# A two-layer encoder on one core: the second layer's transfers leave their queue in the program's order

## The chip, the cores and the metric

The kernel runs on one core of a Trainium2 chip. The metric is the device time of that core in microseconds (us), the median of several runs. The core's engines each run a stream of instructions in order: TensorE (PE, matmuls and transposes), VectorE (DVE), ScalarE (ACT), GpSimd (POOL) and SyncE (SP), which in this kernel does nothing but issue DMA transfers. They meet in semaphores.

## The reference

The program is an encoder trunk of two layers over 1024 tokens of width 1024, in float32. Layer 0 has windowed, dense and memory attention. Layer 1, which the change touches, is cut here to what is computed:

```python
def odd_layer(x, mem_n, table, norm_g, w_in, lq1, lk1, lq2, lk2, subln_g, w_mem_kv, w_out, lam_init):
    h = rmsnorm(x, norm_g)
    q1, q2, k1, k2, v, xq, gate = _split(h @ w_in, ODD_SPLITS)
    ...
    y_c = diff_attention_blocked(q1, q2, k1, k2, v, lam, table)   # p = softmax(s + bias); w = p[0] - lam * p[1]
    y_c = rmsnorm(y_c, subln_g) * (1.0 - lam_init)
    y_x = memory_cross_attention(xq, mem_n, w_mem_kv)
    y = jnp.concatenate([y_c, y_x], axis=-1) * jax.nn.silu(gate)
    return x + y @ w_out
```

There are six differential heads (two score maps of 1024 by 1024 each, a value width of 128) and four memory heads over 256 memory tokens.

## The kernel before, in words

**Precision.** Every float32 operand of a matmul is split into a high part and the rest (suffixes h and l), and each product is three matmuls: high by high, high by low, low by high.

**Stages of layer 1.** `run_steps` (L475 to L530) walks a list of steps: eight cross-attention steps (the ramp, about 635 to 760 us), then six heads of eight query blocks each. One step of a head, over the turns of the loop, is this:

- `s1`: scores `sc` in PSUM, four matmuls of 512 columns (L1505) and four for the low part of k (L1514); one DVE operation (L1520) adds the bias (`toep`) and takes the extremes; ACT takes the exponential (L1523).
- `finish`: DVE normalises the two maps and subtracts them into `e` (L1528, L1530, L1532).
- `hop` (`word_copy`, L565): SP copies `e` to `er`, 512 KB, from SBUF to SBUF, so that it may be read as the matmul's own float type.
- `s2` (L574): eight transposes `te` on PE (L580), whose result ACT (L347) and DVE (L348) split into `PT`.
- `s3`, every second step: `oc`, the product with v (L1545, L1547), added into `O` by ACT and DVE (L1550, L1551); then squares, their sums `ssqc` on PE (L1563), the root on ACT and POOL, `rbcc` on PE (L1576), the scaled `O` on DVE (L1578), the gate on POOL (L1581). The last pair of a head stores its output to `ysc` (`store_y`).

**Filler.** Between these pieces PE runs projection jobs of the next head (k, q, v and gate; `proj_jobs`, matmuls `acc` at L329). A job's 2 x 24 matmuls use one weight block; the block of job i+1 is loaded when job i starts (`load_w`, L235): two transfers `wr` of 256 KB, each cast by DVE into `wh` (L241, 0.5 us) and taken from the raw block by POOL into `wl` (L243, 1.3 us). `wr` has two buffers, which it shares with `wor` and `yr`; `wh` and `wl` have four. A job's results leave through `sg` tiles and small transfers `cq` and `ck`.

**Output weights.** Each turn of the loop also calls `early.step` (L250): it stores the last split piece of the output weights (`wo..h`, `wo..l`), loads the next (`wor`), casts it on ACT (L270) and takes the rest on POOL (L271).

**Tail.** In the last head no projections are left. The output weights come back (`woh`, `wol`, `load_wout`), the stored attention output comes back in chunks `yr` (`y_chunk`, L673), which are split into `yh` by ACT (L350) and `yl` by DVE (L351), and PE's filler is a part of the output projection (`pre`, L702, for token tiles 2, 3 and 4, six of eight k each), whose sums are added to `xh` and stored (`xpsc`). The rest of the output projection follows the loop.

**What sets the order.** The program traces its instructions in the order of the loop. A scheduler then orders every engine's stream by a model of when each instruction could run, inside the dependences; the program can add edges that only order. Nearly all transfers go through one queue, SP's, by the helper `dma` (L175 here, L193 after the change; lines up to L1596 stand 18 lower after the change, those behind it 19 lower).

Of the kernel before, what the change touches and what calls it, by code (L numbers as in the profile page):

```python
# [3 lines left out]

# [1 line left out]

# [82 lines left out]
class Jobs:  # L89
# [59 lines left out]
    def drain(self):  # L149
        self.step = 10 ** 9  # L150
        while self._advance():
            pass


@with_exitstack
def encoder_kernel(ctx, tc, A):
# [76 lines left out]
    def load_w(src, after=None, fast=False):  # L233
        his, los = [], []
        for kh in range(2):  # L235
            raw = wp.tile([P, 4, P], F32, tag="wr", name="wr", bufs=2)
            dma(raw, src[:, 4 * kh:4 * kh + 4, :])
            hi = wp.tile([P, 4, P], F32R, tag="wh", name="wh", bufs=4)
            lo = wp.tile([P, 4, P], F32R, tag="wl", name="wl", bufs=4)
            with (tc.issue_after(after[0]) if after else nullcontext()):  # L240
                nc.vector.tensor_copy(hi, raw)  # L241
            with (tc.issue_after(after[1]) if after else nullcontext()):
                (nc.vector if fast else nc.gpsimd).tensor_tensor(out=lo, in0=raw, in1=hi, op=ALU.subtract)  # L243
            his.append(hi)
            los.append(lo)
        return his, los
# [228 lines left out]
    def run_steps(steps, jobs, hooks=None, pace=None):  # L475
        n = len(steps)
        posts = deque()
        p2 = p3 = 0
        finish = None
        for i in range(n + LAG + 1):  # L480
            behind = None
            if jobs is not None:
                jobs.step = i
            if hooks:
                hooks(i)
            if 0 < i <= n and steps[i - 1].hop:
                steps[i - 1].hop()
            if i < n:
                if steps[i].need:
                    jobs.ensure(*steps[i].need)  # L490
                finish = steps[i].s1()
            f = steps[min(i, n - 1)].fill
            if jobs is not None:
                if half[0] and len(wout) >= 8 and jobs.projected():
                    f = pace(i)
                two = f > 1 and p3 < n and p3 + steps[p3].lag + 1 <= i and steps[p3].s3b is not None
                jobs.pull(f - f // 2 - two)
                if hooks:
                    hooks(-1)
            for q in list(posts):  # L500
                q.pop(0)()
                if not q:
                    posts.remove(q)
            if p3 < n and p3 + steps[p3].lag + 1 <= i:
                st, p3 = steps[p3], p3 + 1
                if st.s3 is not None:
                    if st.need3:
                        jobs.ensure(*st.need3)
                    r = st.s3()
                    if r:  # L510
                        posts.append(r)
                    if st.s3b is not None:
                        jobs.pull(two)
                        st.s3b()
            if p2 < n and p2 + steps[p2].lag <= i:
                behind = steps[p2].s2()
                p2 += 1
            if finish:
                with (tc.issue_after(behind.ins) if behind is not None else nullcontext()):
                    finish()  # L520
                finish = None
            if jobs is not None:
                jobs.pull(f // 2)
                if hooks:
                    hooks(-1)
        while posts:
            for q in list(posts):
                q.pop(0)()
                if not q:
                    posts.remove(q)  # L530
# [276 lines left out]
    last = [None]  # L807
# [185 lines left out]
    jobs = Jobs(jl, ld)  # L993
# [73 lines left out]
    steps = x_steps(M, X, gates, 3, lambda h, qb: (Xq[h], qb * P), 0)  # L1067
# [393 lines left out]
    jobs = Jobs(jl, lambda j: load_w(j["src"], fast=j["tag"] in FAST or j["tag"] == "g7"))  # L1461
# [16 lines left out]
    steps = x_steps(M, X, gates, 3, lambda h, qb: (Xq1[(h, qb // 4)], (qb % 4) * P), 1)  # L1478
# [115 lines left out]
        if i < 0:  # L1594
            wout_hook(1, jobs, "g5", r2)

    run_steps(steps, jobs, hooks1, lambda i: 2)
    jobs.drain()
    left.close()
    st1 = ExitStack()  # L1600
    out_proj(1, None, st1)
# [72 lines left out]
```

## Time and profile before

| | us |
|---|---|
| median of 3 runs | 1228.63 |
| lowest, highest | 1226.69, 1229.92 |
| span of the profiled execution | 1228.9 |
| PE busy | 1196.5 |
| DVE busy | 801.1 |
| ACT busy | 663.1 |
| POOL busy | 436.3 |

The profiled execution has no other time beside its span. It lies 0.3 us above the median. In the rows of the profile an engine's row shows start, duration, line and operation, output and input, and in brackets how long the engine stood idle ahead of it and what ended that. SPq rows are SP's transfers at their issue; PEld are weight loads of PE. A window's row has its length, the busy time and count of PE, PEld, DVE, ACT and POOL, the granted PE clock, the busy share of the DMA engines and the GB/s.

### The profile page before, as it was taken

What the parts mean: (1) busy time and instruction counts of PE and PEld (TensorE: products, weight loads), DVE (VectorE), ACT (ScalarE), POOL (GpSimd) and SP (SyncE); (2) the same over time, 40 slices, a digit from 0 to 9 for tenths busy, and PEclk for the clock granted to TensorE, in tenths of its full rate; (3) what the DMA queues carried; (4) which work ended last, traced back from release to release, by engine and by line L of the source; (5) the groups of instructions that cost most, each with busy time, mean ns of one, the idle gap of its engine ahead of it and who ended that gap; (6) DMA issues with size and microseconds to landing.
All of it is one profiled execution on the core that took longest, in us unless ns stands there. A gap on an engine that the chain in (4) does not pass through costs nothing.

```text
span 1228.9 us, 19560 instructions
## 1 busy us (share of the span) xinstructions
PE 1196.5 (97%) x6614; PEld 988.4 (80%) x6614; DVE 801.1 (65%) x1495; ACT 663.1 (54%) x1477; POOL 436.3 (36%) x414
## 2 busy tenths in 40 slices
PE   6999999999999999999999999999999999999997
PEld 5788888888888777888888777777787777777886
DVE  5547665377778878635365866766767767667544
ACT  6248754366667766636157744555545454445332
POOL 5023365366665455437112222333143231301100
PEclk9999999999999999999999999999999999999999
DMA  6664445545465565457645445355363452468354
GB/s 257 200 194 147 163 172 163 166 160 207 163 233 209 208 227 191 151 196 237 186 158 156 153 146 164 121 183 163 124 187 125 153 171 105 149 212 285 121 192 155
DMA packets 114304, 216.70 MB, mean 176 GB/s; under 512 B 13302, under 2 KB 47478, under 8 KB 114204
## 3 DMA queue, kind: packets, MB, share of 16 engines
q1 hardware_dynamic: 114060, 215.25, 52.5%
q8 instruction: 53, 0.87, 0.3%
q14 instruction: 47, 0.39, 0.1%
q10 hardware_dynamic: 144, 0.20, 0.0%
HBM read 87.71 MB, written 39.86 MB: 104 GB/s over the span
## 4 chain that ended last, share of the span: by engine, by line
PE 47%; DVE 2%; DMA 1%; issue 1%; ACT 1%; POOL 0%; POOLq 0%; SPq 0%; DVEq 0%; ACTq 0%
PE acc L329 24%; PE po L702 5%; PE oc L1545 3%; PE sc L1505 3%; PE te L580 3%; PE sc L1514 2%; PE pre L702 2%; PE oc L1547 2%; DMA wr<-in_w_in 1%; PE ssqc L1563 1%; PE ox L656 0%; PE rbcc L1576 0%; PE tv L439 0%; PE sx L543 0%; DVE e L1520 0%
## 5 line engine op out<-in xcount | busy, mean ns | idle before, releaser
L329 PE MATMUL acc<-h,wh 128*128 128x512 f32 x1536 | 499.5, 398 | 1.6 <-DVE h L351 0.8
L329 PEld LDWEIGHTS acc<-h,wh 128*128 128x128 f32 x1536 | 282.4, 188 | 65.7 <-issue 7.9
L329 PE MATMUL acc<-h,wl 128*128 128x512 f32 x768 | 303.8, 396 | 1.5 <-POOL wl L243 1.2
L243 POOL TENSOR_TENSOR wl<-wr,wh 128x512 fp32r<-128x512 f32 x94 | 124.8, 1329 | 286.3 <-DVE wh L241 155.0
L1523 ACT ACTIVATE e<-e,mn 128x1024 f32<-128x1024 f32 x96 | 110.0, 1148 | 117.0 <-DVE mn L1520 116.9
L329 PEld LDWEIGHTS acc<-h,wl 128*128 128x128 f32 x768 | 144.3, 188 | 34.9 <-issue 4.4
L1114 POOL TENSOR_TENSOR e<-e,rz 128x1024 f32<-128x1024 f32 x48 | 91.6, 1910 | 84.2 <-DVE rz L1113 57.8
L1520 DVE CUSTOM_DVE_ANT_0 e<-sc,toep 128x1024 f32<-128x1024 f32 x96 | 113.5, 1218 | 8.0 <-PE sc L1514 7.3
L580 PEld LDWEIGHTS te<-identr,er 128*128 128x128 f32 x896 | 92.2, 143 | 18.8 <-PE sa L543 2.2
L580 PE MATMUL te<-identr,er 128*128 128x128 f32 x896 | 99.9, 246 | 4.3 <-DVE O L1578 1.4
L348 DVE TENSOR_TENSOR PT<-te,PT 128x512 fp32r<-128x512 f32 x112 | 74.3, 687 | 42.8 <-ACT PT L347 39.2
L241 DVE CAST wh<-wr 128x512 fp32r<-128x512 f32 x112 | 58.2, 522 | 42.9 <-PE acc L329 17.3
L348 DVE TENSOR_TENSOR PTl<-te,PTh 128x512 fp32r<-128x512 f32 x112 | 74.0, 684 | 9.4 <-ACT PTh L347 8.9
L1545 PE MATMUL oc<-PT,v 128*128 128x512 f32 x192 | 69.8, 403 | 0.7 <-DVE ckl L1420 0.7
L1532 DVE SCALAR_TENSOR_TENSOR e<-e,mr 128x1024 f32<-128x1024 f32 x48 | 66.3, 1381 | 1.5
L347 ACT CAST PT<-te 128x512 fp32r<-128x512 f32 x112 | 62.7, 589 | 7.2 <-PE te L580 6.7
L347 ACT CAST PTh<-te 128x512 fp32r<-128x512 f32 x112 | 62.2, 586 | 7.9 <-PE te L580 7.1
L702 PE MATMUL po<-woh,yh 128*128 128x512 f32 (+1 forms) x172 | 65.7, 382 | 0.0
L702 PE MATMUL po<-woh,yl 128*128 128x512 f32 (+1 forms) x172 | 65.5, 381 | 0.0
L702 PE MATMUL po<-wol,yh 128*128 128x512 f32 (+1 forms) x172 | 65.3, 380 | 0.0
L1105 DVE TENSOR_REDUCE mn<-sb 128x1 f32<-128x1024 f32 x48 | 58.3, 1216 | 7.0 <-PE sb L543 6.6
L350 ACT ACTIVATE yh<-yr 128x256 fp32r<-128x256 f32 (+2 forms) x56 | 24.0, 447 | 66.2 <-DMA yr<-ysc 37.5
(211 smaller groups left out, 2358.7 us busy)
## 6 DMA issues: line engine op xcount, KB each, us to landing
er<-e SPq DMA_DIRECT2D x112, 512.0 KB, 3.0
wr<-in_w_in SPq DMA_DIRECT2D x96, 256.0 KB, 3.0
ysc<-gy SPq DMA_DIRECT2D x16, 512.0 KB, 2.7
cq<-sg SPq DMA_DIRECT2D x64, 128.0 KB, 2.5
ck<-sg SPq DMA_DIRECT2D x48, 128.0 KB, 2.3
er<-e SPq DMA_DIRECT2D x12, 384.5 KB, 2.6
xpsc<-xh SPq DMA_DIRECT2D x18, 256.0 KB, 2.6
xr<-xpsc SPq DMA_DIRECT2D x9, 512.0 KB, 3.6
```

The source lines that it names most:

```text
L243: (nc.vector if fast else nc.gpsimd).tensor_tensor(out=lo, in0=raw, in1=hi, op=ALU.subtract)
L329: lastmm[0] = nc.tensor.matmul(acc, a, b[:, k, c0:c0 + n], start=(i == 0), stop=(i == 23))
L347: nc.scalar.copy(hi, src)
L348: return nc.vector.tensor_tensor(out=lo, in0=src, in1=hi, op=ALU.subtract)
L580: nc.tensor.transpose(to[:, i * P:(i + 1) * P], e[0][:, k * P:(k + 1) * P], idt)
L702: lastmm[0] = nc.tensor.matmul(acc, a, b, start=(start and n == 0), stop=(stop and n == 2))
L1105: nc.vector.tensor_reduce(out=mn, in_=Sp, op=ALU.min, axis=AX.X)
L1114: nc.gpsimd.tensor_tensor(out=et, in0=et, in1=rz.to_broadcast([P, 1024]), op=ALU.mult)
L1520: nc.vector.tensor_tensor_reduce(out=et, in0=Sp, in1=toeps[h][:, w0:w0 + 1024], scale=1.0, scalar=BIG, op0=ALU.add, op1=ALU.min, accum_out ...
L1523: nc.scalar.activation(et, et, AF.Exp, bias=mn[:, m:m + 1], scale=-1.0, accum_out=z[:, m:m + 1])
L1532: nc.vector.scalar_tensor_tensor(out=es[0], in0=es[1], scalar=c, in1=es[0], op0=ALU.mult, op1=ALU.add)
L1545: nc.tensor.matmul(acc, V[:, kt, 0, :], ph.both[:, kt, :], start=(kt == 0), stop=(kt == 7), skip_group_check=True)
```

## The change

A helper `in_order` notes the last instruction before its block and, when the block ends, adds an order-only edge from each instruction of the named engines to the one of the same engine that was traced next. Layer 1's loop runs in it, with SP as the only engine. No computation, tile or transfer is changed; the 10457 instructions are the same ones. SP's stream must now be the order of the loop; the other engines are ordered by the scheduler, which sees SP's new order in its model.

```diff
+@contextmanager
+def in_order(tc, engines):
+    bb = tc.nc.cur_bb.bb
+    seen = bb.instructions[-1]
+    yield
+    traced = bb.instructions
+    start = next(k for k in reversed(range(len(traced))) if traced[k] is seen) + 1
+    last = {}
+    for i in traced[start:]:
+        if i.engine not in engines:
+            continue
+        if i.engine in last:
+            tc.add_manual_dep(i, last[i.engine].name,
+                              mybir.DependencyInfo(mybir.DependencyClass.NoSync, mybir.DependencyReason.DATA),
+                              reason="in_order")
+        last[i.engine] = i
...
-    run_steps(steps, jobs, hooks1, lambda i: 2)
-    jobs.drain()
+    with in_order(tc, (mybir.EngineType.SP,)):
+        run_steps(steps, jobs, hooks1, lambda i: 2)
+        jobs.drain()
```

**In a head.** This is SP's stream in the fourth head (about 920 to 955 us), before. The number behind a name is the tile's; `er_10459` and so on are the hops of three successive steps.

```order
L175 DMA er_10459<-e_10362 128x1024
L175 DMA wr_10567<-in_w_in1 128x512
L175 DMA wo11h_119<-wos_10538 128x256
L175 DMA wo11l_120<-wos_10538 128x256
L175 DMA wor_10653<-in_w_out1 128x256
L175 DMA wor_10733<-in_w_out1 128x256
L175 DMA er_10541<-e_10476 128x1024
L175 DMA wo11h_119<-wos_10655 128x256
L175 DMA wo11l_120<-wos_10655 128x256
L175 DMA wr_10758<-in_w_in1 128x512
L175 DMA wr_10764<-in_w_in1 128x512
```

And the same place after the change, between the first and the third of these hops:

```order
L193 DMA er_10459<-e_10362 128x1024
L193 DMA toep_10461<-skew_d_122 128x384
L193 DMA wo11h_119<-wos_10456 128x256
L193 DMA wo11l_120<-wos_10456 128x256
L193 DMA wor_10536<-in_w_out1 128x256
L193 DMA er_10541<-e_10476 128x1024
L193 DMA wr_10561<-in_w_in1 128x512
L193 DMA wr_10567<-in_w_in1 128x512
L193 DMA wo11h_119<-wos_10538 128x256
L193 DMA wo11l_120<-wos_10538 128x256
L193 DMA wor_10653<-in_w_out1 128x256
L193 DMA er_10658<-e_10555 128x1024
```

The weight block 10561/10567 has moved from around the first hop to behind the second, as a pair, and the next one (10758/10764) from behind the second to behind the third. The output weights stand one step nearer to their hop.

On DVE, the place of the casts `wh` of that block, before:

```order
L1520 ISA mn2_10465 128x1
L241 CAST wh_10563<-wr_10561 128x512
L1556 SCALAR_TENSOR_TENSOR es_10818<-mn_10350 128x2
L348 TENSOR_TENSOR PT_10415<-te_10508,PT_10415 128x4x128
L241 CAST wh_10569<-wr_10567 128x512
L348 TENSOR_TENSOR PT_10416<-te_10515,PT_10416 128x4x128
```

After, the two casts stand some ten rows later, behind the scaling of `O` of the pair of blocks before:

```order
L1538 ISA mn2_10544 128x1
L1596 SCALAR_TENSOR_TENSOR O_10408<-O_10408,misc_84,rbcc_10591 128x256
L259 CAST wh_10563<-wr_10561 128x512
L259 CAST wh_10569<-wr_10567 128x512
L1569 TENSOR_TENSOR O_10613<-oc_10596,O_10613 128x256
L366 TENSOR_TENSOR PT_10620<-te_10622,PT_10620 128x4x128
```

They have left the place between the splits of the step before, and stand ahead of the sum `O_10613` and of the splits of this step.

**In the tail.** SP's stream before, around the hop `er_12265` (about 1100 us); the first chunk, `yr_12333`, was issued about 25 rows earlier, just behind `er_11866`.

```order
L175 DMA woh_12147<-wo10h_117 128x512
L175 DMA wol_12148<-wo10l_118 128x512
L175 DMA xh_12345<-x1sc_96 128x512
L175 DMA yr_12351<-ysc1_95 128x4x128
L175 DMA er_12265<-e_12167 128x1024
L175 DMA yr_12357<-ysc1_95 128x2x128
L175 DMA xh_12461<-x1sc_96 128x512
L175 DMA xh_12538<-x1sc_96 128x512
L175 DMA woh_12368<-wo11h_119 128x512
```

After:

```order
L193 DMA er_12265<-e_12167 128x1024
L193 DMA woh_12147<-wo10h_117 128x512
L193 DMA wol_12148<-wo10l_118 128x512
L193 DMA woh_12147<-wo10h_117 128x512
L193 DMA wol_12148<-wo10l_118 128x512
L193 DMA yr_12333<-ysc1_95 128x4x128
L193 DMA yr_12339<-ysc1_95 128x2x128
L193 DMA xh_12345<-x1sc_96 128x512
L193 DMA yr_12351<-ysc1_95 128x4x128
L193 DMA yr_12357<-ysc1_95 128x2x128
L193 DMA woh_12368<-wo11h_119 128x512
```

The first chunk, `yr_12333` and `yr_12339`, has moved behind that hop and behind the last two pairs of the first half of the output weights.

On PE, the first matmuls of `pre` before:

```order
L1563 MATMUL ssqc_12306<-ones2_76,sqc_12220 128x2 x2
L580 MATMUL te_12314<-identr_74,er_12153 128x128 x4
L702 MATMUL pre_12347<-woh_12147,yh_12334 128x512
L702 MATMUL pre_12347<-wol_12148,yh_12334 128x512
L702 MATMUL pre_12347<-woh_12147,yl_12335 128x512
```

After:

```order
L1581 MATMUL ssqc_12306<-ones2_76,sqc_12220 128x2 x2
L598 MATMUL te_12314<-identr_74,er_12153 128x128 x4
L1523 MATMUL sc_12378<-ck0_11585,cq_11941 128x512 x2
L1523 MATMUL sc_12379<-ck1_11586,cq_11944 128x512
L598 MATMUL te_12321<-identr_74,er_12153 128x128 x4
L1523 MATMUL sc_12379<-ck1_11586,cq_11944 128x512
L1532 MATMUL sc_12378<-ckl_11587,cq_11941 128x512
L1532 MATMUL sc_12379<-ckl_11587,cq_11944 128x512
L1532 MATMUL sc_12378<-ckl_11587,cq_11941 128x512
L1532 MATMUL sc_12379<-ckl_11587,cq_11944 128x512
L1594 MATMUL rbcc_12406<-ident_69,rz2_12312 128x128 x2
L598 MATMUL te_12438<-identr_74,er_12265 128x128 x4
```

The first `pre` stands behind these; the second transposes of the block, its scores, `rbcc` and the first transposes of the next hop have moved ahead of it.

More of the change, by code (lines that the diff above doesn't have):

```diff
@@ L2 @@
 from collections import deque
-from contextlib import ExitStack, nullcontext
+from contextlib import ExitStack, contextmanager, nullcontext
 import numpy as np
```

## The prediction

> **What bounds the kernel now.** I read the page first, for which engine is full, then busy time in 20 us windows, for where it is not full.
>
> ```profile
> span 1228.9 us, 19560 instructions
> ...
> PE 1196.5 (97%) x6614; PEld 988.4 (80%) x6614; DVE 801.1 (65%) x1495; ACT 663.1 (54%) x1477; POOL 436.3 (36%) x414
> ```
>
> ```profile
> 760.00:780.00 20.00, 20.00 (x112) 16.04 (x111) 13.85 (x25) 10.00 (x21) 6.93 (x9) 1.00 0.40 135
> 920.00:940.00 20.00, 18.58 (x103) 14.69 (x102) 13.84 (x25) 9.71 (x20) 6.04 (x7) 1.00 0.43 148
> 1100.00:1120.00 20.00, 20.00 (x107) 15.35 (x108) 15.53 (x30) 9.71 (x20) 1.44 (x2) 1.00 0.97 338
> 1120.00:1140.00 20.00, 20.00 (x110) 15.33 (x108) 16.24 (x29) 9.60 (x20) 1.82 (x2) 1.00 0.76 258
> ```
>
> TensorE (PE) is busy in 97% of the span, at the full clock (1.00), and most windows of the second layer's attention look like 760 to 780: no idle time at all. 920 to 940 is the exception, short of 1.42 us. DVE is at 13.8 of 20 us in the middle, but at 15.5 and 16.2 in the tail (1100 to 1140), where the DMA engines are also nearly full for a while (0.97). So a change of one queue's order can gain only what PE waits for today. The table of waits of PE, from 600 to 1165 us (the stretch in which the order changes), has it all:
>
> ```profile
> PE te L580 <- DVE O L1578: 1.4, 1, 1.4
> PE oc L1545 <- DVE ckl L1420: 0.7, 1, 0.7
> PE sx L543 <- DMA xkh<-sg: 0.6, 1, 0.6
> PE rbcc L1576 <- POOL rz L231: 0.5, 1, 0.5
> PE acc L329 <- DVE wl L243: 0.4, 1, 0.4
> PE ox L656 <- DVE mn L1520: 0.4, 1, 0.4
> PE tv L439 <- DVE PT L348: 0.2, 1, 0.2
> PE acc L329 <- DVE gy L460: 0.2, 1, 0.2
> ```
>
> The columns are total, times and longest: eight waits, 4.4 us together. That is the ceiling of a gain, unless PE has slack hidden inside its busy time. The Trainium skill ("Perfetto Trace Analysis", Identifying the Most-Contended Engine) holds that matmul busy time is a bad measure of nearness to the limit and that the share of weight loads is a better one; by the page's 80% of PEld there would be room under the busy time too. This trace can't show such room being opened by SyncE's queue.
>
> **The change part by part.** It removes and adds no instruction. It fixes SP's order to the program's. Where before the scheduler put a transfer as soon as it thought it ready, each now stands behind everything traced ahead of it. Three things come of it.
>
> *First, the longest wait.* How it comes about stands in the chain of waits, then on DVE, then on PE:
>
> ```profile
> 927.94 4.42 DMA wr<-in_w_in
> ```
>
> ```profile
> 932.45 0.43 DVE L241 CAST wh<-wr 128x512 fp32r<-128x512 f32 x1 [2.65 <-DMA wr<-in_w_in]
> ...
> 938.88 0.47 DVE L1578 SCALAR_TENSOR_TENSOR O<-O,misc,rbcc 128x256 f32<-128x256 f32 x1
> 940.60 0.42 DVE L1551 TENSOR_TENSOR O<-oc,O 128x256 f32<-128x256 f32 x1 [1.24 <-ACT O L1550]
> 941.01 1.29 DVE L348 TENSOR_TENSOR PT<-te,PT 128x512 fp32r<-128x512 f32 x2
> ```
>
> ```profile
> 939.41 0.53 PE L580 MATMUL te<-identr,er 128*128 128x128 f32 x4 [1.42 <-DVE O L1578]
> ...
> 947.10 0.50 PE L1563 MATMUL ssqc<-ones,sqc 128*128 128x2 f32 x4
> ```
>
> The second half of a weight block was issued at 927.94 and took 4.42 us; DVE, which runs in order, sat 2.65 us on its cast, all behind it came late, and PE waited 1.42 us for the PSUM tile that L1578 frees. In the new order both halves stand together and, as the rows of DVE show, both casts stand behind L1578. The wait goes: -1.4 us. What is late next is L1551, behind two casts of 0.43 us. Walking SP's queue in the new order with the ready times of this trace, I get the two halves landed at about 939.5 and 941.5, so L1551 would start near 941.9 in place of 940.60, 1.3 us late. The two splits behind it (L348) ended at 942.3; the next user of that PSUM pool on PE is ssqc at 947.10. Those 4.8 us hide the 1.3; if they were gone, it would cost 1.3 in this step, and less in the other pairs, which I get landing 0 to 1.6 us behind L1578.
>
> *Second, weights and e come later in the heads.*
>
> ```profile
> 672.71 2.39 SPq L175 DMA_DIRECT2D cq<-sg  x4
> ```
>
> ```profile
> 936.14 0.48 SPq L175 DMA_DIRECT2D er<-e  x1
> ...
> 938.07 0.94 SPq L175 DMA_DIRECT2D wr<-in_w_in  x2
> ...
> 953.32 0.47 SPq L175 DMA_DIRECT2D er<-e  x1
> ...
> 970.51 1.76 SPq L175 DMA_DIRECT2D ck<-sg  x3
> ```
>
> ```profile
> L243 POOL TENSOR_TENSOR wl<-wr,wh x37: 1276/1289/2377, 702.2 to 1049.0; 128x512 fp32r<-128x512 f32 x37
> ...
> DMA to landing us min/median/max: 2.6/3.2/4.7
> ```
>
> (The last two are from the answer on the weight tile between 700 and 1060 us.) The pair issued at 938.07 now stands behind the er of 953.32: issued at 953.8, some 16 us later, landed 3.2 us after that at 957.0. Two casts of 0.43 and two subtractions of 1.29 end by about 960.5. The job that uses it begins when the job before has been evacuated, and its last stores go out at 970.51: 10 us of cover. So the weights cost nothing, and would cost only if their lateness grew from 16 to 26 us. The er transfers themselves stand behind stores of four pieces (2.39 us of issue) and come 0 to 3.3 us later by my walk. The er of 936.14 lands some 3 us later, and its transposes stand on PE just behind the ssqc of 947.10, which leaves about 8 us: I take zero. In the ramp (the eight cross-attention steps, 635 to 760 us) er moves by 2.5 to 5.5 us and less stands in between: there I bound the cost by 0 and by 2.4 us, one such group of stores, and take 0, since no wait in the table of PE has er as its releaser. The other short waits (0.7, 0.6, 0.4, 0.4, 0.2, 0.2) are taken to stay.
>
> *Third, the tail.* Here PE's filler is the output projection (`pre`, L702), which needs the stored rows yr, their high part yh (ACT L350) and low part yl (DVE L351).
>
> ```profile
> 1065.83 0.38 SPq L175 DMA_DIRECT2D yr<-ysc  x1
> ...
> 1071.87 0.54 SPq L175 DMA_DIRECT2D yr<-ysc  x1
> ...
> 1093.90 0.43 SPq L175 DMA_DIRECT2D woh<-wo10h  x1
> ...
> 1102.13 0.47 SPq L175 DMA_DIRECT2D er<-e  x1
> ...
> 1125.88 1.08 SPq L175 DMA_DIRECT2D yr<-ysc  x2
> ...
> 1137.89 0.47 SPq L175 DMA_DIRECT2D er<-e  x1
> ```
>
> ```profile
> 1105.48 0.63 ACT L350 ACTIVATE yh<-yr 128x512 fp32r<-128x512 f32 x1 [0.21 <-DMA yr<-ysc]
> ```
>
> ```profile
> 1107.13 0.47 PE L702 MATMUL pre<-woh,yh 128*128 128x512 f32 x1
> ```
>
> ```profile
> L702 PE MATMUL pre<-woh,yl x24: 387/397/501, 1107.7 to 1140.8; 128*128 128x512 f32 x24
> ```
>
> ```profile
> L351 DVE SCALAR_TENSOR_TENSOR yl<-yr,yh x12: 272/552/827, 1093.7 to 1156.7; 128x512 fp32r<-128x512 f32 x5, 128x256 fp32r<-128x256 f32 x5, 128x128 fp32r<-128x128 f32 x2
> ...
> DMA to landing us min/median/max: 2.1/3.5/5.2
> ```
>
> The first two yr went out at 1065.83 and 1071.87, long ahead. In the new order they stand behind the er that waits until 1102.13 and four woh/wol transfers at 0.43 us: 1102.13 + 0.47 + 4 x 0.5 gives about 1104.6 for the first and 1105.2 for the second. With the median of 3.5 us they land at 1108.2 and 1108.7; yh takes 0.63, so it stands at about 1109 and 1109.4, against a first `pre` at 1107.13. But the scheduler moves 2.8 us of transposes and scores ahead of `pre` on PE, so PE asks for yh at about 1109.9: just in time. For yl (0.55) DVE, 78% full here, has the queue of its own to clear first; about 1112 against a third matmul near 1110.6: a loss of about 1.0 after the PE work that stands between. The second place is token tile 4, whose `pre` begins when 24 triples are through, at about 1141.1. Its yr go from 1125.88 to behind the er of 1137.89, so about 1138.4; landed 1141.9, split 1142.5, loss 1.4. Together 2.4 us; the ends are 0.5 (landing in 2.1 us) and 5 (landing in 5.2 at both places, 2 x 1.7 more, less what is in between). I take the middle, by the median. PE's late start then brings the tail's rbcc wait (0.5, its releaser on POOL) down to about 0.1: -0.4.
>
> The sum, against this execution: 1228.9 - 1.4 + 0 + 0 + 2.4 - 0.4 = 1229.5. The execution's span is 0.3 above the median of the runs shown, 1228.6, so the forecast is 1229.2, which is no change. About 0.3% (3.7 us) is what a measurement of this kernel can tell from none.
>
> **The rivals.**
>
> *A: the tail is the bound (slower).* The place is 1104 to 1145 us. If the yr land as the slowest rows do (5.2 us), since two pairs of woh/wol and an er are ahead of them on DMA engines that stand at 0.97, and yl then has to queue on a DVE with 3.8 to 4.5 us free in 20, both starts of `pre` slip by 1.7 us more and DVE's critical chain in the tail by another 0.7: 2.4 + 3.4 + 0.7 = 6.5, less 1.8: 1233.3. It decides the sign once the tail loses more than 5.5 us. For it: DMA 0.97; against: the woh that made the 0.97 are mostly later than the yr. Chance 0.17. The Trainium skill speaks for this side ("DMA: Bandwidth & Descriptors", Rules for kernel authors): issue a transfer early and wait for it late. The trace agrees in the tail, where the two early yr never made PE wait.
>
> *B: the casts become a wait of their own (slower).* Twenty-odd pairs of casts now stand between L1578 and L1551. If the second half landed over 4.8 us behind L1578, PE would stop at ssqc or te in each such step, near 1 us apiece; five of them give 1228.6 - 1.8 + 2.4 + 5 = 1234. Against it: the landing of 2.6 to 4.7 us and a queue that is empty most of the time. Chance 0.05.
>
> *C: a real gain.* The tail costs nothing (yr in time as PE's own order moved), and the other waits go as well: 1228.6 - 4.4 = 1224.2. Only the 1.4, and through the moved instructions perhaps the 0.5 and the 0.7, can hang on SP's order, so the likelier form is -1.4 - 0.5 - 0.7: 1226.0, within the 0.3%. Faster than that: 0.08.
>
> *D: the change doesn't do what it says.* SP's rows do stand in another order, so no chance of its own; time 1228.6.
>
> **How the numbers follow.** The forecast, with the tail anywhere between 0.5 and 5 and the mild form of C, has 0.70: 1226.0 to 1231.8. A and B have 0.22, C's strong form 0.08. Faster by over 0.3% 0.08, within it 0.70, slower 0.22. The range leaves out the strong form of C and what of A and B lies above 1233.5: 1226.0 to 1233.5.
>
> **What would show it.** Right: PE without the wait near 939; the wr in pairs some 16 us later with no PE wait for wh or wl; the first yr issued near 1105, a PE wait of 1 to 2 us for yl near 1110 and one near 1141. Wrong: PE waits for te or oc in most heads (B); a tail that loses over 5 us (A); or PE windows of the heads that hold more matmuls than now (room under the busy time).

## The result, and the profile after

The changed kernel takes 1239.62 us (median of 4 runs, 1238.55 to 1240.27) against 1227.95 us for the kernel before on the same chip: 1.0094 times the time, interval 1.008 to 1.0108. It is slower by 11.7 us, outside the range that was forecast.

PE is as busy as it was, the span is 7.9 us longer:

```profile
span 1236.8 us, 19538 instructions
...
PE 1198.5 (97%) x6614; PEld 985.7 (80%) x6614; DVE 807.1 (65%) x1495; ACT 661.8 (54%) x1477; POOL 437.6 (35%) x414
```

The spans alone mislead here, because the profiled execution of before took some 4 us more in layer 0, which the change doesn't touch; 3.4 of them are the clock (last section). A span is also about 1.8 us shorter than the time of the same execution (1236.8 and 1238.55 us here), so spans compare with spans only. So I compare the stretch that changed, by the start of the same matmul in both traces: the 1243rd `acc` matmul (before 615.61), the 2485th (before 1103.69) and the 238th `po` matmul of the final projection (before 1164.11).

| us | ramp and heads | tail | together |
|---|---|---|---|
| before | 488.1 | 60.4 | 548.5 |
| changed | 497.9 | 62.9 | 560.7 |
| difference | +9.8 | +2.5 | +12.2 |

The four longest groups of PE's waits in the changed kernel, from 560 us on:

```profile
PE te L598 <- ACT z L1585: 7.6, 10, 1.5
PE pre L720 <- ACT yh L368: 1.3, 2, 0.7
PE sx L561 <- DMA xkh<-sg: 0.8, 1, 0.8
PE rbcc L1594 <- POOL rz L249: 0.5, 1, 0.5
```

The 1.4 us wait behind L1578 is gone, as forecast, and so is that for `ckl`. In their place `te` waits ten times for ScalarE's `z`, 7.6 us, which in this stretch of the kernel before it never did. `z` reads the PSUM tile `ssqc`, from the pool that `te` takes its tile from. The loads on which the engines ahead of `z` waited, in the heads (670 to 1105 us), VectorE's and ScalarE's rows, first before and then after:

```profile
DVE wh L241 <- DMA wr<-in_w_in: 9.8, 8, 2.7
ACT wos L270 <- DMA wor<-in_w_out: 13.7, 9, 2.5
```

```profile
DVE wh L259 <- DMA wr<-in_w_in: 26.7, 27, 2.9
ACT wos L288 <- DMA wor<-in_w_out: 20.0, 13, 6.0
```

Both engines stand longer at weight loads: VectorE at 27 casts in place of 8, ScalarE for up to 6.0 us at once. One step shows how small a delay is enough. Before, the end of `z` and the second group of transposes (ScalarE's row, then PE's):

```profile
827.60 0.41 ACT L1567 ACTIVATE z<-ssqc,es 128x1 f32<-128x1 f32 x2 [0.27 <-PE ssqc L1563]
```

```profile
828.31 0.45 PE L580 MATMUL te<-identr,er 128*128 128x128 f32 x4
```

`z` ended at 828.01 and `te` began at 828.31: 0.3 us to spare. The same step in the changed kernel, on SP, DVE, ACT and PE:

```profile
817.26 0.48 SPq L193 DMA_DIRECT2D er<-e  x1
817.79 3.01 SPq L193 DMA_DIRECT2D wr<-in_w_in  x2
```

```profile
821.75 0.42 DVE L259 CAST wh<-wr 128x512 fp32r<-128x512 f32 x1
822.09 0.68 DVE L366 TENSOR_TENSOR PT<-te,PT 128x512 fp32r<-128x512 f32 x1
823.07 0.81 DVE L259 CAST wh<-wr 128x512 fp32r<-128x512 f32 x1 [0.30 <-DMA wr<-in_w_in]
823.80 0.68 DVE L366 TENSOR_TENSOR PT<-te,PT 128x512 fp32r<-128x512 f32 x1
...
827.03 1.21 DVE L1538 CUSTOM_DVE_ANT_0 e<-sc,toep 128x1024 f32<-128x1024 f32 x1
```

```profile
830.58 0.39 ACT L1585 ACTIVATE z<-ssqc,es 128x1 f32<-128x1 f32 x2
```

```profile
831.02 0.54 PE L598 MATMUL te<-identr,er 128*128 128x128 f32 x4 [0.39 <-ACT z L1585]
```

The weights stand behind `er`, and one cast has come to stand between the two splits `PT`, whose result the chain needs: `PT`, then `e`, the next scores' minimum (L1538), two exponentials on ScalarE, `z`, `te`. A wait of 0.30 us and a cast of 0.81 in that chain are more than the 0.3 to spare. The first step of the first head shows the other engine (SP's rows, then ScalarE's, then PE's):

```profile
710.38 1.92 SPq L193 DMA_DIRECT2D wr<-in_w_in  x2
...
715.34 0.33 SPq L193 DMA_DIRECT2D wor<-in_w_out  x1
```

```profile
717.61 0.41 ACT L288 CAST wos<-wor 128x256 fp32r<-128x256 f32 x1 [5.98 <-DMA wor<-in_w_out]
717.92 0.37 ACT L1568 COPY O<-oc 128x256 f32<-128x256 f32 x1
```

```profile
726.19 0.54 PE L598 MATMUL te<-identr,er 128*128 128x128 f32 x4 [1.46 <-ACT z L1585]
```

`wor` went out 5 us behind the weight pair; ScalarE, in order, stood 5.98 us at its cast, with its part of `O` and `PT` behind it.

The two engines don't share the loss evenly. I followed each of the nine waits for `z` in the heads (7.1 us) back, from `z` to what released it or to what stood ahead of it on its engine, as far as the last transfer that was waited for. Eight of them (5.7 us) come to a cast `wh` that waited for `wr`, and only that of 726.19 (1.46 us) to `wos`. The casts themselves are longer too: 14 of 42 took over 0.6 us in the heads, against 3 of 41 before.

### The profile page after: what moved, and what is told of

Its sections match the earlier page's. It is cut to its first block, busy times and chain, and to the rows that moved or that the text cites. A ratio compares the mean times of both kernels' runs of the same rounds, so it can differ in the third digit from the quotient of the medians.

```text
span 1236.8 us, 19538 instructions
## 1 busy us (share of the span) xinstructions
PE 1198.5 (97%) x6614; PEld 985.7 (80%) x6614; DVE 807.1 (65%) x1495; ACT 661.8 (54%) x1477; POOL 437.6 (35%) x414
## 4 chain that ended last, share of the span: by engine, by line
PE 31%; DMA 7%; DVE 5%; ACT 4%; issue 3%; SPq 3%; POOL 1%; POOLq 0%; ACTq 0%; DVEq 0%
PE acc L347 15%; PE po L720 5%; DMA wr<-in_w_in 4%; SPq L193 3%; PE sc L1523 2%; PE oc L1563 2%; PE pre L720 2%; PE te L598 2%; PE sc L1532 2%; DMA wor<-in_w_out 2%; PE oc L1565 1%; DVE wh L259 1%; DVE PT L366 1%; DVE e L1550 1%; ACT e L1541 1%
## 5 line engine op out<-in xcount | busy, mean ns | idle before, releaser
L1538 DVE CUSTOM_DVE_ANT_0 e<-sc,toep 128x1024 f32<-128x1024 f32 x96 | 113.6, 1217 | 8.1 <-PE sc L1532 7.8
L598 PE MATMUL te<-identr,er 128*128 128x128 f32 x896 | 100.7, 246 | 10.3 <-ACT z L1585 7.6
L259 DVE CAST wh<-wr 128x512 fp32r<-128x512 f32 x112 | 67.1, 603 | 57.2 <-DMA wr<-in_w_in 35.3
L1550 DVE SCALAR_TENSOR_TENSOR e<-e,mr 128x1024 f32<-128x1024 f32 x48 | 62.0, 1292 | 1.4
L249 POOL TENSOR_TENSOR rz<-z,nhalf 128x2 f32<-128x2 f32 x24 | 16.7, 696 | 130.6 <-ACT z L1585 90.0
```

What stands on the lines that cost most here:

```text
L598: nc.tensor.transpose(to[:, i * P:(i + 1) * P], e[0][:, k * P:(k + 1) * P], idt)
L1538: nc.vector.tensor_tensor_reduce(out=et, in0=Sp, in1=toeps[h][:, w0:w0 + 1024], scale=1.0, scalar=BIG, op0=ALU.add, op1=ALU.min, accum_out ...
L1550: nc.vector.scalar_tensor_tensor(out=es[0], in0=es[1], scalar=c, in1=es[0], op0=ALU.mult, op1=ALU.add)
```

## The experiments

The runs are named e1 to e15. Heads and tail below are the stretches of the table above, so 488.1 and 60.4 before, 497.9 and 62.9 changed. "Left out of the chain" means that the scheduler places these transfers. To do so, `dma` notes a kind for each transfer, and `in_order` passes over the kinds named:

```diff
-        (eng or nc.sync).dma_start(out=out, in_=in_)
+        h = (eng or nc.sync).dma_start(out=out, in_=in_)
+        KIND[h.ins.name] = kind
...
-        if i.engine not in engines:
+        if i.engine not in engines or KIND.get(i.name) in LOOSE:
```

The kernel before had medians of 1226.37 us beside the first four runs, 1226.06 beside the next four, 1226.65 and 1226.0 beside the later ones. The changed kernel itself was not timed again beside them; by its ratio it would be at about 1237.8.

One thing in these stretches is not in the waits. In some of the profiled executions PE's granted clock fell to half for 3.4 us, which is worth 1.7 us (last section): once in the heads of the changed kernel and of e2, e3, e4, e5, e10 and e12, twice in those of e9, once in the tail of e3, and not at all in the heads and tails of the other runs. So a difference of 1.7 us between two stretches can be this alone.

**Which transfers?** First, the weight loads left out (e1): `LOOSE = ("wr",)`.

> The changed kernel, but the weight loads (wr) are left out of the chain: the scheduler places them, all other transfers of the loop stay in traced order. Theory 1 (the pair of weight halves lands behind its place in the order of VectorE; the casts wait, and the whole step of VectorE, ScalarE's z and with it the transposes te come late): the casts wait for wr about 10 us in the stretch as before (29.6 us in the changed kernel), te waits for z under 1 us (7.6), time 1229 to 1232, the tail's 2.5 us remain. Theory 2 (er and the small stores, standing behind each other, are late, and the weights only go along): te still waits 6 to 8 us, time 1238 to 1240.

Measured: 1234.05 us, 1.0057 (1.0036 to 1.0078); heads 491.4, tail 63.0; `te` waits for `z` 4.3 us. Two thirds of the heads' loss went (6.5 us, of which the fall of the clock is 1.7), a third stayed: neither theory's number.

The tail's transfers left out (e2): `LOOSE = ("yr",)`, the kind that yr, woh, wol, xh and xpsc were given.

> The changed kernel, but the tail's transfers (yr, woh, wol, xh, xpsc) are left out of the chain. Both theories: the heads keep their loss, the two waits of pre for yh (1.3 us) go, time 1236 to 1238, that is 2 to 3 us under the changed kernel. If the tail is bound by VectorE and not by yr, the time stays at 1239 to 1240.

Measured: 1237.76 us, 1.0091 (1.0064 to 1.0118). The time says little, the stretches say it: heads 498.3, tail 60.1, and no wait of `pre` is left. The tail's loss is the order of these transfers, 2.8 us.

Only `wr` and `er` held (e4): `KIND.get(i.name) not in ("wr", "er")`.

> Only wr and er are held in traced order (wr behind the er that is traced ahead of it); the stores, output weights, toep and the tail are the scheduler's. Theory 1: the heads' loss is here with this alone, time 1234 to 1238, casts wait for wr 20 us or more. Theory 2 (the stores and output weights ahead of er make the loss): time 1227 to 1230, te waits for z under 1 us.

Measured: 1231.58 us, 1.0045 (1.0029 to 1.0062); heads 491.6, tail 60.3. This alone costs 3.6 us in the heads, 1.7 of them by the clock, less than theory 1 expected, and the casts' waits were 15.8 us.

The output weights left out (e5): `LOOSE = ("wor",)` (loads and stores).

> The changed kernel with the pieces of the output weights (wor and their stores) left out of the chain; wr, er, the small stores, toep and the tail stay in traced order. Theory 3 (two in-order engines each stand at a late load: VectorE's casts at wr, ScalarE's casts wos at wor, and either makes z and te late): the heads recover about a third to two thirds of their 9.8 us, waits of wos for wor fall from 20 towards 13 us, te waits for z 3 to 5 us, time 1231 to 1235 where the changed kernel is at about 1238 beside these runs. Theory 1 alone (wr only): no recovery, 1237 to 1239.

Measured: 1236.06 us, 1.0079 (1.0059 to 1.01); heads 493.3, tail 63.2. A part came back in the heads (4.6 us), though the time is over the range.

Both kinds of weights left out (e6): `LOOSE = ("wr", "wor")`.

> The changed kernel with both kinds of weight loads (wr, wor and wor's stores) left out of the chain. Theory 3: the heads are as before, te waits for z under 1 us, only the tail's 2.5 us are left, time 1228 to 1230 beside a kernel before of about 1226.4. Theory 2 (er behind the small stores of q and k): te still waits 3 us or more, time 1231 or over.

Measured: 1228.9 us, 1.0029 (1.0017 to 1.0041); heads 485.8, tail 63.4. In the heads (670 to 1105 us) one wait is left of all:

```profile
PE oc L1568 <- DVE ckl L1443: 0.7, 1, 0.7
```

Theory 2 falls with it: er, the small stores and toep are held in traced order here and cost nothing. What is left in the time, 2.8 us, is the tail's 3.0.

The tail left out as well (e7): `LOOSE = ("wr", "wor", "yr")`.

> As the one before, and the tail's transfers are left out too: in traced order stay only er, the small stores of q and k, toep and the outputs. Theory 3: no loss is left, 1225 to 1228, the same as the kernel before within 0.2%. Theory 2: 1229 or over.

Measured: 1225.38 us, 0.9996 (0.9986 to 1.0005); heads 486.8, tail 60.2. All is back. So the whole loss is in three kinds of transfers.

Only `er` and the output weights held (e8).

> Only er, wor and wor's stores are held in traced order; wr, the small stores, toep and the tail are the scheduler's. Theory 3: this alone costs 2 to 5 us in the heads, by ScalarE's wait for wor and z behind it: 1228 to 1231. If wor has no part of its own: 1226 to 1227.

Measured: 1226.14 us, 1.0001 (0.9992 to 1.0011); heads 486.6. Held output weights alone cost nothing, though ScalarE waited up to 5.0 us at once for them: against theory 3 in this form. In e1, with all but `wr` in order, 3.3 us are left in the heads; what makes the difference was not tested.

**By which engine?** The changed order, but the casts `wh` on GpSimd in the loop (e3): `(nc.gpsimd if pool_cast[0] else nc.vector).tensor_copy(hi, raw)`.

> The changed kernel with its order of transfers, but in the loop the casts wh run on GpSimd and not on VectorE. Theory 1: VectorE no longer stands behind the landing of wr, te waits for z under 2 us, time 1230 to 1234 (GpSimd's longer queue may give waits of rbcc for rz, up to 2 us). Theory 2: te still waits 6 to 8 us, time 1238 to 1241.

Measured: 1238.06 us, 1.0095 (1.0074 to 1.0117); heads 495.5, tail 66.1. Of the tail, 1.7 us are the clock. Theory 1 as the only cause falls: no cast of the loop is on VectorE, and in the heads

```profile
PE te L599 <- ACT z L1586: 6.5, 8, 1.8
```

```profile
ACT wos L288 <- DMA wor<-in_w_out: 28.7, 18, 6.5
```

ScalarE now waits 28.7 us for `wor`, longer than in the changed kernel (20.0): with the casts on GpSimd `wor` comes later still, so this run shows ScalarE's place larger than it is there. The obvious next step was to let `wor` go too: the casts on GpSimd and `LOOSE = ("wor",)` (e9).

> The changed kernel with the output weights (wor, its stores) out of the chain and the casts wh on GpSimd: no engine on the way to z stands behind a weight load that is held. Theory 3 (VectorE's place behind wr and ScalarE's behind wor are the two causes): te waits for z under 1 us, heads within 1 us of before, time 1228 to 1230 with the tail's loss. If GpSimd's longer use of the port that it shares with VectorE is what made the casts on GpSimd useless: te still waits 3 us or more, 1232 to 1237.

Measured: 1235.15 us, 1.0067 (1.005 to 1.0083); heads 494.5, tail 64.0; `te` still waits for `z` 6.4 us. Theory 3 failed as it was put, and the trace says why. SP, POOL, ACT and PE in its first head:

```profile
708.46 1.30 SPq L197 DMA_DIRECT2D wr<-in_w_in  x2
...
715.78 2.25 SPq L197 DMA_DIRECT2D wor<-in_w_out  x2
```

```profile
714.47 1.28 POOL L266 TENSOR_TENSOR wl<-wr,wh 128x512 fp32r<-128x512 f32 x1
```

```profile
717.87 0.41 ACT L293 CAST wos<-wor 128x256 fp32r<-128x256 f32 x1 [7.71 <-DMA wor<-in_w_out]
```

```profile
726.46 0.75 PE L604 MATMUL te<-identr,er 128*128 128x128 f32 x4 [3.10 <-ACT z L1591]
```

`wor` is free of the chain, and yet goes out at 715.78, just when GpSimd has subtracted the first half of the pair (714.47 + 1.28 = 715.75). `wor` and `wr` share two buffers: a weight pair that comes late keeps them late, whatever the queue. The casts on GpSimd have a part in it here, since GpSimd itself waits at them for `wr`, up to 10.3 us at once. That is theory 4. To test it, `wor` got a buffer of its own (e12; the kilobyte came from the second `sqc` buffer):

```diff
-                raw = wp.tile([P, 512], F32, tag="wr", name="wor", bufs=2)[:, 0:256]
+                raw = wp.tile([P, 256], F32, tag="worx", name="wor", bufs=1)
-                    sq = M.pl.tile([P, 256], F32, tag="sq", name="sqc", bufs=2)
+                    sq = M.pl.tile([P, 256], F32, tag="sq", name="sqc", bufs=1)
```

> The changed kernel with its order of transfers; wor gets a buffer of its own (1 KB of a partition, paid for by one of the two sqc buffers) in place of one of the two that it shares with wr. Theory 4 (a weight pair that is held in order keeps both shared buffers until GpSimd has subtracted it, wor then lands late, and ScalarE stands at its cast wos ahead of its part of O and PT): ScalarE waits for wor under 10 us (20.0 in the changed kernel) and never over 3 us at once (6.0), the heads recover 4 to 8 of their 9.8 us, time 1230 to 1235 beside a kernel before at about 1226.5; the casts' waits for wr stay. If the shared buffer has no part: 1237 to 1240.

Measured: 1239.97 us, 1.0111 (1.0096 to 1.0126); heads 498.4, tail 62.9. Nothing came back: taken away alone, the shared buffer is not it either. ScalarE's wait for `wor` fell to 14.5 us (5.3 at most), near the 13.7 of before, but VectorE's casts still stand in the chain. Both together, the buffer of e12 and the casts of e3 (e13):

> As e12, and the casts wh on GpSimd: neither ScalarE behind wor's buffer nor VectorE behind wr. Theory 3 and 4 together (these two waits are the whole of the heads' loss): te waits for z under 1 us, heads within 1.5 us of before, time 1228 to 1231 with the tail's 2.5 us. If GpSimd's port or queue makes a loss of its own: 1232 to 1237.

Measured: 1231.55 us, 1.0044 (1.0028 to 1.0059); heads 488.3, tail 64.2. The heads are back within 0.3 us of before, with all transfers still in traced order; what remains of the waits of `te` is

```profile
PE te L599 <- ACT z L1586: 2.4, 5, 0.7
```

ScalarE still waits 18.7 us for `wor` here, 4.2 at most, and none of these five waits comes from there: they lead to the last operation of `finish` on VectorE (L1551 here), which took 1.5 to 2.4 us beside GpSimd's work in place of 1.28. So the sum of an engine's waits doesn't measure the loss; it counts where little room stands behind them. The tail (waits of `pre` of 2.1 us) makes up the rest. Their control, the kernel before with the buffer of e12 (e14):

> Control: the kernel before with wor's own buffer and one sqc buffer, no chain. 1225 to 1227.5 by all theories; what it differs by from the kernel before is taken off e12.

Measured: 1228.44 us, 1.0012 (1.0003 to 1.0022); heads 489.0, tail 60.2, slower than expected. The edit itself costs 0.9 us in the heads: `te` waits three times for `z`, 2.5 us, and all three lead to `wos`, two of them to its wait for `wor`. That is ScalarE's place at work with no transfer held in order. Against this control e12 still loses 9.4 us in the heads, and e13 nothing.

**Is it the PSUM slot?** `te` waits for `z` only because `ssqc` sits in its pool. The changed kernel with `T = ps_a("ssqc")` in place of `ps_t` (e10):

> The changed kernel with its order of transfers, but ssqc takes its PSUM tile from the pool of acc and not from that of te, so that no te can wait for the z that reads it. If the slot is how the lateness reaches TensorE: te waits for z 0, the heads recover more than half of their 9.8 us, time 1230 to 1234 (other waits, for acc or for PT, may take up to 2 us). If the lateness is in the loop e, er, te, PT itself and the slot only names it: other te waits of about the same sum, 1236 to 1239.

Measured: 1240.19 us, 1.0112 (1.0093 to 1.013); heads 496.7. The waits of `te` for `z` are gone, and others stand in their place:

```profile
PE tv L457 <- DVE PT L366: 3.1, 4, 1.1
PE pre L720 <- ACT yh L368: 2.2, 2, 1.5
PE ssqc L1581 <- DVE ckl L1438: 2.1, 1, 2.1
PE ssqc L1581 <- DVE sg L369: 2.0, 1, 2.0
```

The two of `ssqc` are for a slot again, now of `acc`, which DVE empties late. The late chain itself is the loss; the slot only gives it a name. The same edit in the kernel before, where nothing is late (e11):

> The kernel before with the same move of ssqc to the pool of acc, no chain. te stands 0.3 us behind z in the kernel before without waiting, so little is to be had: 1225 to 1227, the same as before; the 1.42 us wait of te for O (L1578 reads rbcc, in the pool of te still) stays unless the order moves. Over 1228 if acc then waits for z.

Measured: 1224.75 us, 0.9981 (0.997 to 0.9991); heads 484.5. The 1.4 us wait is gone, the casts wait 4.6 us for `wr` in place of 9.8, and this version is a little faster than either kernel. Why the order comes out better was not followed. With the harmless part of the chain on top (that of e7; e15):

> The best found so far put together: er, the small stores, toep and outputs in traced order, both weights and the tail left to the scheduler, ssqc in the pool of acc. Each part had 0.998 to 1.000 of the time before: 1223 to 1226 if they add, 1226 to 1228 if they hinder each other.

Measured: 1224.62 us, 0.9987 (0.9977 to 0.9998); heads 484.4, tail 61.3. The parts don't add: it is no faster than with the move of `ssqc` alone.

## Why the prediction was wrong, point by point

**The longest wait: right.** The 1.4 us of 939 are gone, and the casts stand where the order had them. VectorE's longest wait for wr was 2.9 us. But the heads, forecast at -1.4 us in all, measured +9.8.

**The cover of the casts: this step failed.** The prediction hid 1.3 us of lateness of L1551 behind 4.8 us, counted to "the next user of that PSUM pool on PE", `ssqc`. That user had room. But the late DVE chain goes on through `e`, the minimum, two exponentials and `z`. In the very step that the prediction walked, the room there was 0.06 us: `z` ended at 948.40 and `te` began at 948.46.

```profile
948.01 0.39 ACT L1567 ACTIVATE z<-ssqc,es 128x1 f32<-128x1 f32 x2
```

```profile
948.46 0.55 PE L580 MATMUL te<-identr,er 128*128 128x128 f32 x4
```

After the change PE is 2.2 us later at this place, and the sum on DVE (L1551, now L1569) starts 2.7 us later, so it is late by 0.5 us against PE and not by 1.3; the second cast, priced at 0.43, took 1.52. That was enough for a wait of `te`:

```profile
941.88 1.52 DVE L259 CAST wh<-wr 128x512 fp32r<-128x512 f32 x1 [0.19 <-DMA wr<-in_w_in]
943.32 0.41 DVE L1569 TENSOR_TENSOR O<-oc,O 128x256 f32<-128x256 f32 x1
```

```profile
951.08 0.54 PE L598 MATMUL te<-identr,er 128*128 128x128 f32 x4 [0.32 <-ACT z L1585]
```

I read the cover at the first engine that would meet the delay and not along the chain to the last.

**The weights: this step failed too.** "10 us of cover", and so a cost of zero, was the cover of the matmuls that use the weights. As such it was right: the pair that went out at 938.07 goes out some 15 us later (the trace is about 2 us behind there),

```profile
955.30 1.31 SPq L193 DMA_DIRECT2D wr<-in_w_in  x2
```

and no PE wait for `wh` or `wl` is among the longer rows above. But the engines that prepare a weight stand at it in order, and what is behind them doesn't have the weights' cover. VectorE's casts are one such place; ScalarE's cast of `wor` is the other, and the prediction didn't see it at all, since `wor` comes late through a buffer shared with `wr`, which no queue shows. Taking one place away alone didn't bring the heads back: e3 (the first gone, the second made worse) has +7.4 us in the heads, e12 (the second back to the size of before) +10.3, e13 (both edits) +0.2. In the changed kernel itself the first place carries most of the waits, 5.7 of 7.1 us. The heads came out at +9.8 with the 1.4 gained, so the terms taken as zero measured about +11, of which 1.7 are the clock.

**er and the ramp: right.** er and the small stores held in order cost nothing (e6, e7), and the ramp lost under 1 us up to 696 us. There the ramp ends: the last `ox` of the kernel before starts at 695.8, and the 760 of the prediction is wrong.

**The tail: right in place and near in size, wrong in the part that waits.** Forecast 2.4 less 0.4, measured 2.5; yr at 1104.6 forecast, and 1110.90 in a trace that was 5.8 us later by then:

```profile
1107.90 0.47 SPq L193 DMA_DIRECT2D er<-e  x1
...
1110.90 0.93 SPq L193 DMA_DIRECT2D yr<-ysc  x2
...
1145.34 0.96 SPq L193 DMA_DIRECT2D yr<-ysc  x2
```

```profile
1116.74 0.50 PE L720 MATMUL pre<-woh,yh 128*128 128x512 f32 x1 [0.67 <-ACT yh L368]
...
1149.53 0.50 PE L720 MATMUL pre<-woh,yh 128*128 128x512 f32 x1 [0.67 <-ACT yh L368]
```

Both starts of `pre` wait, for `yh` and not for `yl`, 0.67 us each where 1.0 and 1.4 were forecast; the rbcc wait stayed at 0.5, so the 0.4 taken off was wrong. A wait of `te` for `z` at 1148.32 (0.46 us) that nobody forecast brings the sum up, so the nearness of the size is in part luck. The Trainium skill's rule that was set beside rival A ("DMA: Bandwidth & Descriptors", Rules for kernel authors: issue early, wait late) agrees with these losses: the weights, the output weights and the yr all went out later.

**The rivals.** B was the nearest: casts that become a wait of their own, with `te` as the place where PE stops. It had 0.05, since I made it decide only past 4.8 us of lateness; delays of 0.5 us and more were enough. It had the place of eight of the nine waits in the heads, and not ScalarE's.

**What stays open.** Of the 12.2 us, the waits of PE give 7.3 (11.7 against 4.4) and the fall of the clock (below) 1.7. In the starts of the matmuls each wait costs about 0.05 to 0.25 us more than its row says; I put it at 1.7 for ten. Some 1.5 us I can't put to rows. Why the clock fell here and not in the heads before is not shown either. Why held output weights cost 3.3 us in e1 and nothing in e8 was not tested: it fits that the free `wr` then waits for buffers which a late `wor` keeps, but no run takes that alone. Nor was it tested why e5 got 4.6 us back and e12 none, though both leave the casts behind held `wr`; e5 frees the stores of the output weights too.

## What to carry to other kernels

The cover of a late load is not that of its last user: it is the shortest along every in-order engine that touches the load on the way, with all that stands behind that instruction. Look also at whom it shares buffers with; a transfer that nobody holds can still be held by a buffer. When one suspect is removed and nothing moves, test it together with the next before dropping either.

## What the runs showed of the hardware

The granted clock of PE fell to half behind one of the waits of the changed kernel (windows of 1 us; PEclk is the third value from the end), which cost 0.41 + 0.50 + 0.50 + 0.29 = 1.7 us:

```profile
992.00:993.00 1.00, 1.00 (x6) 0.90 (x7) 0.65 (x1) 1.00 (x3) 0.92 (x2) 0.59 0.76 311
993.00:994.00 1.00, 1.00 (x4) 0.81 (x3) 0.81 (x3) 0.14 (x1) 0.43 (x1) 0.50 0.00 0
994.00:995.00 1.00, 1.00 (x3) 0.72 (x3) 0.00 (x0) 0.56 (x1) 0.00 (x0) 0.50 0.00 0
995.00:996.00 1.00, 1.00 (x5) 0.81 (x4) 0.89 (x3) 0.04 (x1) 0.00 (x0) 0.71 0.00 0
```

The wait ahead of it had been 1.24 us. Falls of the same depth and length, to 0.50 for 3.4 us, stand in the heads or tails of seven more traces (at 994 in e2, 727 and 1151 in e3, 726 in e4, 748 in e5, 726 and 750 in e9, 729 in e10, 673 in e12), each within 1.5 us of a wait of PE of 1.35 to 3.1 us, but for the one in e12, which stands behind two of 0.8 and 0.5. Not every such wait had one: none stands behind 1.51 us at 749 in the changed kernel, 1.47 us at 989 in e1 and 2.42 us at 995 in e12. The profiled execution of before had two falls in layer 0 (0.67 and 0.66 in the 5 us from 420 and from 440), where the changed kernel's has none: so two spans of this kernel can differ by 3.4 us for this alone, and stretches have to be compared. The Trainium skill ("TensorE: Matmul & The Clock Gate", Why this matters for your kernels) puts the fall behind idle gaps of over about 3 us; the row here has it behind a shorter one.

The second cast of an adjacent pair can also take longer than 0.43 us, next to GpSimd's subtraction of the first, which then takes longer too (2.21 us here, 1.29 in most rows):

```profile
741.62 2.21 POOL L261 TENSOR_TENSOR wl<-wr,wh 128x512 fp32r<-128x512 f32 x1 [6.39 <-DVE wh L259]
```

```profile
742.60 1.52 DVE L259 CAST wh<-wr 128x512 fp32r<-128x512 f32 x1
```
